# The four down projections of a diffusion backbone by seven products of quarter blocks instead of eight, the sums for them on GpSimd

## The chip, the cores and the metric

The program runs on one core of a Trainium2 chip. The metric is the device time of one launch in microseconds. The kernel before was timed in three runs, the kernel after is timed the same way. One further execution of the kernel before was taken with the hardware profiler; all rows below come from that one.

## The reference, cut to what matters

The model has two layers of three sub-layers each. The first and the last of a layer are SwiGLU blocks, the middle one is a mixer (in layer 0 a recurrence beside windowed attention, in layer 1 dense attention). The tokens are 512 latent tokens and 256 context tokens; the last sub-layer needs the 512 latent ones alone. D is 1024, D_FF 2816.

```
def _ffn_sublayer(h, shift, scale, gate, g_pre, g_post, w_gate, w_up, w_down):
    u = _modulate(_rmsnorm(h, g_pre), shift, scale)
    y = (jax.nn.silu(u @ w_gate) * (u @ w_up)) @ w_down
    return h + FFN_RES * gate * _rmsnorm(y, g_post)
...
for l in range(DEPTH):                      # DEPTH = 2
    x  = _ffn_sublayer(x, ..., ffn_w_gate[l, 0], ffn_w_up[l, 0], ffn_w_down[l, 0])
    xc = _ffn_sublayer(xc, ...)             # the context tokens, with the same weights
    x, xc = x + mixer..., xc + mixer...
    x  = _ffn_sublayer(x, ..., ffn_w_gate[l, 1], ffn_w_up[l, 1], ffn_w_down[l, 1])
    if not last: xc = _ffn_sublayer(xc, ...)
```

All is float32. The change concerns the four products `@ w_down` ([tokens, 2816] by [2816, 1024]); what prepares them is moved into the time of the products with `w_gate` and `w_up` just before.

## The kernel before, in words

The six sub-layers run one after the other, s = 0 to 5; s = 0, 2, 3 and 5 are the SwiGLU blocks. Tokens come in two chunks: 2 x 384 in s = 0, 2 and 3, 2 x 256 in s = 5.

A float32 product is three float32r passes on TensorE. Each operand is split into hi (a copy on ScalarE, ACT) and lo (the difference, on VectorE, DVE: a subtraction with both inputs in SBUF, lines L193 and L725), and hi*hi + hi*lo + lo*hi is summed in PSUM.

`ffn` is one SwiGLU block. The first two feature tiles (128 features each) are plain products (L200 to L202, `gu`). The other 20 are made by `strassen`, two tiles (a pair) at a time: for gate and for up one `job` of seven products (banks `px`, `py`, `pz`, L601), 84 matmuls. A job's weights (`w`, two loads of 512 KB on SyncE's queue, SP) are split, and sums of them are made on DVE (L614 to L617) and split again. DVE adds the products to what ACT has copied (L634), ACT applies Silu, DVE multiplies (L638). The finished pair h goes to DRAM (`hd<-h`).

The down projection is `type2`: 22 k-tiles; for each, w_down's 128 rows (512 KB) and a tile of h (`hr`) come from SP's queue and are split, and each token tile takes six matmuls of 512 columns (L701, accumulators `d000a` to `d110a`: layer, block, chunk, a). In s = 0, 2 and 3 it goes chunk by chunk; in s = 5 all four token tiles go together. The last four k-tiles (STAG) are done tile by tile, so that one token tile is finished while the others still run. For a finished tile, `boundary` takes the squares on ACT and the product with the gate G on DVE (L506), and makes 1/rms, its power step on GpSimd (POOL, L210); its `rest` loads x (a DMA on POOL's queue, L512), adds (DVE, L514), stores x (POOL's queue, L518) and calls `make_u`: POOL scales (L414), TensorE transposes (L419, `utp`), DVE and ACT modulate (L393, L395) and split (L193) into the next sub-layer's u. Where the next sub-layer is a SwiGLU block, `Sums` also makes four sums of u, half of them on POOL (L437, L451 and L453: operations with two inputs in SBUF) and half on DVE (L450, L452). The rests of the first chunk's tiles run beside the second chunk's products; those of the second chunk's run at the start of the next sub-layer.

What sets the order: each engine runs its instructions in a fixed order, which a scheduler makes from the order of the program and from when buffers come free. DMAs stand in the queue of the engine that issues them: one that waits holds up what stands behind it. Buffers that matter here: `raw` (weights as loaded) 3, hi and lo of weights 8 each, `c3` 23 slots of 3 KB a partition, `G0` and `G1` (the two gates, loaded before the down projection) one each, `by` 3, `junk` 1. PSUM has eight banks, of which the phases of the kernel (`psum_phase`) take six or eight.

## Time and profile before

| | us |
|---|---|
| median of three runs | 2626.99 (2625.99 to 2627.03) |
| span of the profiled execution | 2636.3 |
| TensorE (PE) busy in the span | 2546.2, 97% |
| VectorE (DVE) busy | 1757.5, 67% |
| ScalarE (ACT) busy | 1351.8, 51% |
| GpSimd (POOL) busy | 325.3, 12% |

The profiled execution is 9.3 us longer than the median of the timed runs. The stages of it that the change touches, in us from the start of the span: gate and up at 78 to 393, 981 to 1273, 1513 to 1804 and 2312 to 2501; down at 393 to 583, 1273 to 1463, 1804 to 1994 and 2501 to 2625. "Busy" is the time in which an engine executes instructions; an engine can be 67% busy on the mean and 99% in one stage, so rows are read by stage. "Idle before" is an engine's idle time ahead of an instruction, and the name after the arrow is what ended it.

### The profile page before, as it was taken

How to read it: one execution, taken by the hardware profiler on the slowest of the kernel's cores; microseconds unless marked ns; L12 is line 12 of the kernel's file. 1: busy time of each engine (PE TensorE's matmuls, PEld its weight loads, DVE VectorE, ACT ScalarE, POOL GpSimd, SP SyncE). 2: the span in 40 equal slices, each digit the busy share in tenths (PEclk: the TensorE clock that was granted, in tenths of full speed). 3: DMA queues.
4: the chain of work that ended last, by engine and by line, in shares of the span. 5: the costliest groups of instructions: out<-in, count | busy, mean ns of one | idle time of the engine just before them, and what ended most of it. 6: DMA issues, size and time to landing. Idle time of an engine off the chain costs nothing.

```text
span 2636.3 us, 38740 instructions
## 1 busy us (share of the span) xinstructions
PE 2546.2 (97%) x13980; PEld 2237.5 (85%) x13980; DVE 1757.5 (67%) x3199; ACT 1351.8 (51%) x2783; POOL 325.3 (12%) x356
## 2 busy tenths in 40 slices
PE   7999999999999999999999999999999899899998
PEld 5899998889855789999888899998887667799986
DVE  5766664658777686767555767665557657899843
ACT  4444444547566654444454544444545556666632
POOL 4000000213022240000011300000122221400000
PEclk8999999999999999999999999999999999999999
DMA  7445436541387443232555332235554552544542
GB/s 275 144 160 168 152 127 206 192 160 53 119 293 266 157 141 96 96 105 100 187 184 189 124 97 95 98 107 177 198 181 152 200 176 82 177 135 128 161 167 88
DMA packets 147761, 403.00 MB, mean 153 GB/s; under 512 B 16504, under 2 KB 33576, under 8 KB 147568
## 3 DMA queue, kind: packets, MB, share of 16 engines
q1 hardware_dynamic: 136688, 362.00, 41.6%
q0 software_dynamic: 10880, 38.53, 4.2%
q8 instruction: 109, 1.79, 0.3%
q14 instruction: 84, 0.69, 0.1%
HBM read 351.91 MB, written 48.55 MB: 152 GB/s over the span
## 4 chain that ended last, share of the span: by engine, by line
PE 80%; DVE 7%; issue 5%; ACT 3%; POOL 3%; DMA 2%; POOLq 0%; DVEq 0%; ACTq 0%; SPq 0%
PE px L601 17%; PE py L601 12%; PE pz L601 12%; PE d110a L701 4%; PE d100a L701 4%; PE d000a L701 4%; PE d010a L701 4%; PE ada L122 3%; PE d001a L701 3%; PE d101a L701 3%; PE eo0a L701 1%; PE oq1a L701 1%; PE qkv1a L701 1%; PE opT L1286 1%; PE gu L201 1%
## 5 line engine op out<-in xcount | busy, mean ns | idle before, releaser
L210 POOL TENSOR_TENSOR b_0pr<-b_0pv,mhalf 128x1 f32<-128x1 f32 x4 | 2.2, 560 | 983.9 <-DVE b_0pv L208 983.9
L634 DVE TENSOR_TENSOR cp<-px,cp 128x384 f32<-128x384 f32 (+1 forms) x160 | 76.5, 520 | 56.3 <-PE px L601 56.3
L724 ACT ACTIVATE hh<-hr 128x384 fp32r<-128x384 f32 x132 | 68.6, 521 | 81.5 <-DMA hr<-hd 80.6
L725 DVE TENSOR_TENSOR hh<-hr,hh 128x384 fp32r<-128x384 f32 x132 | 72.9, 559 | 50.6 <-ACT hh L724 49.5
L636 ACT ACTIVATE h<-cp 128x384 f32<-128x384 f32 (+1 forms) x160 | 77.0, 498 | 26.1 <-DVE cp L634 21.9
L122 PE MATMUL ada<-wa,sc 128*32 128x512 f32 x512 | 83.8, 611 | 0.5 <-DVE cols L137 0.4
L634 DVE TENSOR_TENSOR cp<-pz,cp 128x384 f32<-128x384 f32 (+1 forms) x80 | 41.9, 524 | 57.4 <-PE pz L601 56.4
L638 DVE TENSOR_TENSOR h<-cp,h 128x384 f32<-128x384 f32 (+1 forms) x160 | 79.6, 519 | 0.4
L629 ACT ACTIVATE cp<-px 128x384 f32<-128x384 f32 (+1 forms) x160 | 71.4, 446 | 0.0
L634 DVE TENSOR_TENSOR cp<-py,cp 128x384 f32<-128x384 f32 (+1 forms) x80 | 41.7, 521 | 26.7 <-PE py L601 17.2
L614 DVE TENSOR_TENSOR w<-w,w 128x512 f32<-128x512 f32 x80 | 56.8, 709 | 1.6 <-DMA w<-in_wgu_dram 0.2
L193 DVE TENSOR_TENSOR d110w_0lo<-d110w,d110w_0hi 128x512 fp32r<-128x512 f32 x22 | 15.2, 691 | 63.6 <-ACT d110w_0hi L193 63.6
L617 DVE TENSOR_TENSOR w<-w,w 128x512 f32<-128x512 f32 x80 | 55.3, 691 | 2.0
L615 DVE TENSOR_TENSOR w<-w 128x512 f32<-128x512 f32 x80 | 55.2, 690 | 1.9
L616 DVE TENSOR_TENSOR w<-w,w 128x512 f32<-128x512 f32 x80 | 55.1, 689 | 1.5
L701 PE MATMUL d011a<-d011w_0hi,hh 128*128 128x512 f32 x132 | 52.7, 399 | 0.2 <-ACT hh L724 0.2
L701 PE MATMUL d101a<-d101w_0hi,hh 128*128 128x512 f32 x132 | 52.5, 398 | 0.0
L701 PE MATMUL d001a<-d001w_0hi,hh 128*128 128x512 f32 x132 | 52.5, 398 | 0.0
L701 PE MATMUL d100a<-d100w_512hi,hh 128*128 128x512 f32 x132 | 52.4, 397 | 0.0
L701 PE MATMUL d000a<-d000w_512hi,hh 128*128 128x512 f32 x132 | 52.4, 397 | 0.0
L701 PE MATMUL d010a<-d010w_0hi,hh 128*128 128x512 f32 x132 | 52.3, 396 | 0.0
L701 PE MATMUL d101a<-d101w_512hi,hh 128*128 128x512 f32 x132 | 52.2, 396 | 0.0
(5579 smaller groups left out, 9579.9 us busy)
## 6 DMA issues: line engine op xcount, KB each, us to landing
w<-in_wgu_dram SPq DMA_DIRECT2D x175, 512.0 KB, 3.5
wa<-in_w_ada_dram SPq DMA_DIRECT2D x204, 256.0 KB, 4.6
hd<-h SPq DMA_DIRECT2D x66, 384.0 KB, 4.7
hr<-hd SPq DMA_DIRECT2D x132, 192.0 KB, 3.7
wa<-in_w_ada_dram SPq DMA_DIRECT2D x42, 512.0 KB, 4.3
d000w<-in_w_down_dram SPq DMA_DIRECT2D x22, 512.0 KB, 3.5
d001w<-in_w_down_dram SPq DMA_DIRECT2D x22, 512.0 KB, 3.8
d010w<-in_w_down_dram SPq DMA_DIRECT2D x22, 512.0 KB, 3.9
```

What stands on the lines that cost most here:

```text
L122: ins = nc.tensor.matmul(acc[32 * g:32 * g + 32, :], lhsT=self.sc[:, k, :], rhs=raws[g], start=(k == 0), stop=(k == KD - 1), skip_group_ch ...
L601: mm = lambda x, y, **kw: nc.tensor.matmul(out, lhsT=x, rhs=y, skip_group_check=True, **kw)
L614: nc.vector.tensor_sub(x3, x1, x3)
L615: nc.vector.tensor_add(x1, x1, x2)
L617: nc.vector.tensor_sub(x4, x4, x2)
L629: nc.scalar.activation(t, src, AF.Copy)
L634: nc.vector.tensor_add(t, acc, t)
L636: nc.scalar.activation(hc, t, AF.Silu)
L638: nc.vector.tensor_mul(hc, t, hc)
L701: mm(acc[:, h:min(h + 512, n)], lhsT=x[xi][:, js], rhs=w[h // 512][wi], start=(k == 0 and xi == 0 and wi == 0), stop=(k == nk - 1 and xi = ...
L724: self.nc.scalar.activation(t[:, 0], src, AF.Copy)
L725: self.nc.vector.tensor_sub(t[:, 1], src, t[:, 0].bitcast(F32))
```

## The change

A pair of feature tiles of h, by the two chunks of tokens, is a block of 2 x 2: a11 and a21 are the first tile's features for the first and second chunk, a12 and a22 the second tile's. The two tiles' rows of w_down, by halves of 512 columns, are the other: b11, b12 the first tile's, b21, b22 the second's. The result has four quarters (chunk by half of D). The old way needs eight products of such blocks, the new seven (Strassen's scheme in Winograd's form), each summed over the 11 pairs.

- `down_sums` loads a pair's rows of w_down a second time (into the places of `G0` and `G1`) during gate and up, makes b12 - b11, b22 - b12, b22 - b12 + b11 and b21 less that by four POOL subtractions of 128x512, and stores them (two DMAs of 512 KB on POOL's queue) to `wt` in DRAM.
- `h_sums` makes a21 + a22, a11 - a21, a21 + a22 - a11 and a12 less that by four POOL operations of 128x384 (128x256 in s = 5) and stores them with three DMAs on POOL's queue; a12 and a22 are stored by SP. Before, SP stored both tiles.
- `down` is new: seven products, each of 11 pairs by m token tiles (3, or 2 in s = 5) by three matmuls of 512 columns. Weights and h are loaded two pairs at a time. Of the PSUM banks, products 1, 3, 6 and 7 use `dx` and products 2, 4 and 5 `dy`; partial results are copied to SBUF by ACT (`keep`) and added by DVE (`add`, one input in PSUM). In products 6 and 7 the lo halves of h are made on POOL for two of three loads.
- `boundary` is split: `half` is done for each half of D when it is ready, `end` makes 1/rms. The first chunk's left half is ready after product 2, its right half after product 5; the rests of the first chunk run during products 6 and 7. The second chunk's tiles are finished in product 7, STAG now counts pairs.
- In s = 5 the down projection also goes by the two chunks of 256 tokens.

```
+    def down_sums(self, l, s, p, wt):
+        b = [self.bp.tile([P, D], F32, tag=f"G{e}", name=f"wt{l}{s}{p}{e}") for e in range(2)]
+        for e in range(2):
+            nc.sync.dma_start(b[e], self.a["w_down"][l, s, (2 * p + e) * P:(2 * p + e + 1) * P, :])
+        (b11, b12), (b21, b22) = ((x[:, 0:512], x[:, 512:]) for x in b)
+        sub = nc.gpsimd.tensor_sub
+        sub(b11, b12, b11)
+        sub(b12, b22, b12)
+        nc.gpsimd.dma_start(wt[p, 0], b[0])
+        sub(b22, b22, b11)
+        sub(b21, b21, b22)
+        nc.gpsimd.dma_start(wt[p, 1], b[1])
+
+    def h_sums(self, h, n, hd, nm):
+        a11, a21, a12, a22 = (x[:, c * n:(c + 1) * n] for x in h for c in range(2))
+        nc.sync.dma_start(hd[1], h[1])
+        s12 = self.bp.tile([P, 2, n], F32, tag="by", bufs=3, name=f"hs{nm}")
+        s4 = self.junk(f"hs{nm}")[:, 0:n]
+        nc.gpsimd.tensor_add(s12[:, 0], a21, a22)
+        nc.gpsimd.tensor_sub(a21, a11, a21)
+        nc.gpsimd.dma_start(hd[0], h[0])
+        nc.gpsimd.tensor_sub(s12[:, 1], s12[:, 0], a11)
+        nc.gpsimd.dma_start(hd[2], s12.rearrange("p c n -> p (c n)"))
+        nc.gpsimd.tensor_sub(s4, a12, s12[:, 1])
+        nc.gpsimd.dma_start(hd[3][:, 0:n], s4)
...
+        def product(a, b, acc, first, done):
...
+            for p in range(np_):
+                if i > 4 and p % 2 and self.later:
+                    self.later.pop(0)()
...
+                if p % 2 == 0:
+                    w = min(2, np_ - p)
...
+                    br = self.ws.tile([P, w, 512], F32, tag="raw", bufs=3, name=f"dw{nm}{p}")
+                    nc.sync.dma_start(br, b(q))
+                    ar = self.c3([P, w, n], F32, f"dh{nm}{p}")
+                    nc.sync.dma_start(ar, a(q))
...
+                    self.halves(ah, al, ar, nc.gpsimd if i > 4 and p % 4 else nc.vector)
+                wh, wl = self.split(br[:, p % 2], f"dw{nm}{p}s")
...
+        product(blk(0, 0), raw(0, 0), x, True, keep(u1))
+        product(blk(1, 0), raw(1, 0), y, True, add(u1, left))
...
+        product(blk(2, 1), mod(1, 1), x, False, keep(u2))
...
+        product(blk(2, 0), mod(0, 0), z, True, keep(c22))
+        product(blk(3, 0), raw(1, 1), z, False, add(u2, right))
+        product(blk(0, 1), mod(0, 1), x, False, add(c22))
+        product(blk(1, 1), mod(1, 0), x, False, second)
...
         for p in range(1, NF // 2):
             h = [self.c3([P, 2 * n], F32, f"h{l}{s}_{2 * p + e}") for e in range(2)]
+            self.down_sums(l, s, p, wt)
             for b in range(2):
                 job(p, b, h)
-            for e in range(2):
-                nc.sync.dma_start(hd[2 * p + e], h[e])
-        self.psum_phase(joint)
+            self.h_sums(h, n, hd[p], f"{l}{s}{p}")
```

What this does to the order of POOL's instructions in the last sub-layer's gate and up: before, POOL made the last sums of u there (L451, L453 for token tile 5) and after them had only the gates' load and the down projection's boundaries.

```order
L451 TENSOR_TENSOR b4_5y_21756<-b4_5uut_21779 128x512
L453 TENSOR_TENSOR b11_5_21620<-b11_5_21620,b01_5_21619 128x512
L167 DMA G17_0_24908<-gd17_20986 128x1024
L210 TENSOR_TENSOR b5_2pr_25732<-b5_2pv_25730,mhalf_71 128x1
L512 DMA b5_4x_25818<-xd4_19063 128x1024
```

After, at the same place (pairs are numbered in the names: `hs110` and `hd11` are the sums of h's pair 0 and their place in DRAM, `wt1120` and `wt1121` the two weight tiles of pair 2):

```order
L607 DMA hd11_22160<-hs110_22459 128x512
L608 TENSOR_TENSOR hs110q_22460<-h11_1_22254,hs110_22459 128x256
L609 DMA hd11_22160<-hs110q_22460 128x256
L588 TENSOR_TENSOR wt1120_22776<-wt1120_22776 128x512
L589 TENSOR_TENSOR wt1120_22776<-wt1121_22777,wt1120_22776 128x512
L590 DMA wt11_22161<-wt1120_22776 128x1024
L591 TENSOR_TENSOR wt1121_22777<-wt1121_22777,wt1120_22776 128x512
L592 TENSOR_TENSOR wt1121_22777<-wt1121_22777 128x512
L593 DMA wt11_22161<-wt1121_22777 128x1024
L588 TENSOR_TENSOR wt1130_23074<-wt1130_23074 128x512
```

So POOL now holds a chain of subtractions and stores for each pair. The scheduler puts the weight sums early: those of pairs 0 and 1 stand ahead of the first sums of h, and in each of the next pairs two follow, so that nine of the eleven are made in the first half of the stage. The other three SwiGLU blocks have the same pattern, there starting beside the boundary work of the mixer or block before.

On SP's queue in the same stage, before (`w113`, `w114` are the gate and up weights of pairs 3 and 4, `hd11<-h11_4` a store of h):

```order
L174 DMA w11310_22803<-in_wgu_dram 128x1024
L174 DMA w11311_22805<-in_wgu_dram 128x1024
L662 DMA hd11_21806<-h11_4_22383 128x512
L174 DMA w11400_22945<-in_wgu_dram 128x1024
L662 DMA hd11_21806<-h11_5_22384 128x512
L174 DMA w11401_22947<-in_wgu_dram 128x1024
```

and after:

```order
L174 DMA w11310_23222<-in_wgu_dram 128x1024
L585 DMA wt1150_23670<-in_w_down_dram 128x1024
L585 DMA wt1151_23671<-in_w_down_dram 128x1024
L174 DMA w11311_23224<-in_wgu_dram 128x1024
L174 DMA w11400_23382<-in_wgu_dram 128x1024
L585 DMA wt1160_23968<-in_w_down_dram 128x1024
L600 DMA hd11_22160<-h11_5_22775 128x512
L585 DMA wt1161_23969<-in_w_down_dram 128x1024
L174 DMA w11401_23384<-in_wgu_dram 128x1024
```

Loads of gate and up weights (`w11311`, `w11401`) now stand behind loads of `wt`, and a load of `wt` can only start when POOL's store of the weight sums before it has left the same buffer.

## Rows read from the trace of the kernel before

**Rows 1.** The page: busy time by engine, and the chain's shares by engine
```profile
PE 2546.2 (97%) x13980; PEld 2237.5 (85%) x13980; DVE 1757.5 (67%) x3199; ACT 1351.8 (51%) x2783; POOL 325.3 (12%) x356
...
PE 80%; DVE 7%; issue 5%; ACT 3%; POOL 3%; DMA 2%; POOLq 0%; DVEq 0%; ACTq 0%; SPq 0%
```
**Rows 2.** Stretches start:end; each engine's busy us; PEclk, DMA share, GB/s
```profile
393.00:485.00 92.00, 92.00 (x396) 74.13 (x395) 48.95 (x86) 42.12 (x82) 2.08 (x3) 1.00 0.59 192
1365.00:1463.00 98.00, 96.56 (x430) 77.62 (x429) 57.41 (x99) 50.08 (x102) 25.27 (x25) 1.00 0.56 185
2501.00:2625.00 124.00, 123.41 (x528) 99.07 (x528) 47.13 (x80) 37.07 (x71) 2.84 (x5) 1.00 0.40 135
```
**Rows 3.** Stretches with gate and up; columns PE, PEld, DVE, ACT, POOL
```profile
1513.00:1804.00 291.00, 291.00 (x1649) 291.00 (x1649) 196.80 (x330) 137.74 (x258) 0.00 (x0) 1.00 0.30 99
2270.00:2300.00 30.00, 25.79 (x213) 24.89 (x212) 26.16 (x53) 16.97 (x42) 15.68 (x15) 1.00 0.46 150
2300.00:2501.00 201.00, 198.53 (x1679) 197.72 (x1678) 183.29 (x343) 129.60 (x268) 0.00 (x0) 1.00 0.44 139
2312.00:2332.00 20.00, 20.00 (x172) 20.00 (x171) 18.64 (x35) 12.93 (x28) 0.00 (x0) 1.00 0.47 148
```
**Rows 4.** POOL's timeline in three places: start us, us, instruction
```profile
66.23 2.23 POOL L483 TENSOR_TENSOR zt<-zt,zt 128x768 f32<-128x768 f32 x1 [1.96 <-DVE zt L482]
...
945.27 1.33 POOL L453 TENSOR_TENSOR b<-b,b 128x512 f32<-128x512 f32 x1
...
961.79 3.37 POOL L451 TENSOR_TENSOR b_5y<-b_5uut 128x512 f32<-128x512 f32 x1 [0.93 <-DVE b_5uut L393]
```
**Rows 5.** DVE's timeline in the same three places
```profile
66.68 2.34 DVE L614 TENSOR_TENSOR w<-w,w 128x512 f32<-128x512 f32 x1
...
945.38 0.69 DVE L506 TENSOR_TENSOR b_5y<-eo1a,G 128x512 f32<-128x512 f32 x1
...
962.12 1.29 DVE L193 TENSOR_TENSOR u_1l<-b_5uut,u_1h 128x512 fp32r<-128x512 f32 x2
963.33 0.69 DVE L452 TENSOR_TENSOR b<-b_5uut,b_5y 128x512 f32<-128x512 f32 x1
```
**Rows 6.** Single lines, ns minimum/median/maximum of one, first and last start
```profile
L193 DVE TENSOR_TENSOR d011w_0lo<-d011w,d011w_0hi x22: 674/692/1781, 1361.6 to 1444.9; 128x512 fp32r<-128x512 f32 x22
L453 POOL TENSOR_TENSOR b<-b,b x8: 1262/1286/1409, 945.3 to 2290.7; 128x512 f32<-128x512 f32 x8
L437 POOL TENSOR_TENSOR b<-u_0h,u_0l x16: 1282/1596/2876, 910.9 to 2258.8; 128x512 f32<-128x512 f32 x16
```
**Rows 7.** DVE's additions from PSUM by form, 2312 to 2491
```profile
L634 DVE TENSOR_TENSOR cp<-px,cp 128x256 f32<-128x256 f32 x38 | 14.4, 420 | 3.1 <-PE px L601 3.1
L634 DVE TENSOR_TENSOR cp<-pz,cp 128x256 f32<-128x256 f32 x18 | 7.6, 421 | 1.0
L634 DVE TENSOR_TENSOR cp<-py,cp 128x256 f32<-128x256 f32 x18 | 7.5, 418 | 0.0
```
**Rows 8.** Two stretches of 10 us behind the third sub-layer's down projection
```profile
1473.00:1483.00 10.00, 6.75 (x37) 6.42 (x36) 6.69 (x10) 2.76 (x6) 6.52 (x6) 0.88 0.51 188
1493.00:1503.00 10.00, 10.00 (x59) 10.00 (x58) 9.96 (x24) 6.75 (x18) 0.00 (x0) 1.00 0.25 98
```
**Rows 9.** PE's waits at 1463 to 1513: total us, times, longest
```profile
PE b_5utp L419 <- POOL b_5y L414: 3.2, 1, 3.2
```
**Rows 10.** The chain there: start us, us, what
```profile
1464.56 1.21 DVE b_4x L514
...
1475.16 1.29 DVE b_5x L514
...
1481.67 1.97 PE b_5utp L419 x8
```
**Rows 11.** DMA issues: KB each, median us to landing; a store's time on POOL
```profile
w<-in_wgu_dram SPq DMA_DIRECT2D x175, 512.0 KB, 3.5
hd<-h SPq DMA_DIRECT2D x66, 384.0 KB, 4.7
hr<-hd SPq DMA_DIRECT2D x132, 192.0 KB, 3.7
xd<-b_2x POOLq DMA_DIRECT2D x5, 512.0 KB, 3.0
...
1455.48 0.59 POOL L518 DMA_DIRECT2D xd<-b_3x  x1 [1.62 <-DVE b_3x L514]
```

More of the change, by code (lines that the diff above doesn't have):

```diff
@@ L521, in boundary, with half, end, rest @@
-        return rest
+        def half(i, y):
+            nc.scalar.activation(junk[:, cut[i]], y, AF.Square, accum_out=ss[:, i:i + 1])
+            nc.vector.tensor_mul(y1[:, cut[i]], y, g[:, cut[i]])
+        def end():
+            nc.vector.tensor_add(ss[:, 0:1], ss[:, 0:1], ss[:, 1:2])
+            r = self.rms_r(ss[:, 0:1], D, name + "p")
+            def rest():
+                x = bp.tile([P, D], F32, tag="bx", bufs=2, name=name + "x")
+                nc.gpsimd.dma_start(x, xsrc(t))
+                for c in cut if nxt is None else [slice(0, D)]:
+                    nc.vector.scalar_tensor_tensor(x[:, c], y1[:, c], r[:, 0:1], x[:, c], op0=ALU.mult, op1=ALU.add)
+                    if nxt is None:
+                        nc.sync.dma_start(xdst(t)[:, c], x[:, c])
+                if nxt is not None:
+                    nc.gpsimd.dma_start(xdst(t), x)
+                    self.make_u(x, y1, t, *nxt, name + "u")
+            return rest
@@ L524, in ffn_weights, with ffn @@
+        return half, end
     def ffn_weights(self, l, s, f):
         return [self.weights(self.a["wgu"][l, s, f, b], f"w{l}{s}{f}{b}") for b in range(2)]
-    def ffn(self, l, s, u, sums, tiles, gate, finish, hook=None, joint=False):
+    def ffn(self, l, s, u, sums, tiles, gate, start, finish, hook=None, joint=False):
         nc = self.nc
         n = len(tiles[0]) * P
-        hd = self.dp.tile([NF, P, 2 * n], F32, name=f"hd{l}{s}")
+        hd = self.dp.tile([NF // 2, 4, P, 2 * n], F32, name=f"hd{l}{s}")
+        wt = self.dp.tile([NF // 2, 2, P, D], F32, name=f"wt{l}{s}")
@@ L567, in ffn @@
                     sums.most()
[L568 to L570 removed]
+        self.down_sums(l, s, 0, wt)
+        self.h_sums([h[0], h[1]], n, hd[0], f"{l}{s}0")
+        self.strassen(l, s, u, sums, n, hd, wt, joint)
         self.flush()
[L572 to L586 removed]
@@ L588, in strassen @@
-    def strassen(self, l, s, u, sums, n, hd, joint):
+        self.down(l, s, n, hd, wt, self.load_gate(*gate), start, finish, hook)
+    def down_sums(self, l, s, p, wt):
+        nc = self.nc
+        b = [self.bp.tile([P, D], F32, tag=f"G{e}", name=f"wt{l}{s}{p}{e}") for e in range(2)]
[9 more added lines that the diff above has]
+        nc.gpsimd.dma_start(wt[p, 1], b[1])
@@ L591, in strassen @@
+    def strassen(self, l, s, u, sums, n, hd, wt, joint):
         nc = self.nc
@@ L1335, in fin @@
                     self.later.append(sn.prepare)
+            def fin(c, j, acc, g, start=start, finish=finish):
+                half, end = start(c, j, g)
+                for i in range(2):
+                    half(i, acc[:, i * 512:(i + 1) * 512])
+                finish(c, j, end)
             if sub == 1:
@@ L1338, in body @@
             else:
-                self.ffn(l, sub // 2, u, sums, tl[s], gate, fin, {0: self.even_consts, 3: self.odd_consts}.get(s), s == 5)
+                self.ffn(l, sub // 2, u, sums, tl[s], gate, start, finish, {0: self.even_consts, 3: self.odd_consts}.get(s), s == 5)
             u, sums, xsrc = un, sn, dst
```

102 lines of the change are left out of this document (66 added, 36 removed).

## The prediction

> **What bounds the kernel now.** I read the page first: PE is busy 97% of the span, DVE 67%, POOL 12%, and PE holds 80% of the chain that ended last [rows 1]. So PE's matmuls set the time on the mean. Then I read the windows of the stages that the change touches. In a down projection PE is full (92.00 of 92.00 us for 396 matmuls; 123.41 of 124.00 for 528 in the last sub-layer) and DVE half idle [rows 2]. In gate and up with 384 tokens a chunk PE is again full and DVE at 196.80 of 291.00 us, POOL at nothing. But in the last sub-layer, with 256 tokens, DVE has 183.29 of 201 us, and 18.64 of 20 in one pair of feature tiles: there PE and DVE are nearly level, and the pair has no room [rows 3]. What the reader is to see is that the change takes work from PE in stages where PE alone is the bound, and puts POOL work into stages in one of which the bound is almost DVE. Last I read what POOL's two-input operations do to DVE, in three places.
>
> **Removed matmuls.** A sub-layer's down projection with 768 tokens has 22 x 6 x 6 = 792 matmuls of 512 columns; the seven products have 7 x 11 x 3 x 3 = 693, so 99 fewer. At 92.00/396 = 0.232 us [rows 2] this is 23.0 us, three times. The last has 528, then 7 x 11 x 2 x 3 = 462: 66 x 0.234 = 15.4 us. Together -84.4 us. It counts in full, since PE has no idle time there. The cover needed in its place: two pairs bring 512 KB of weights and 256 KB of h in 12 matmuls, 2.8 us, in the last sub-layer, that is 280 GB/s; the same stretch moved 135 GB/s at a DMA share of 0.40 [rows 2], so 0.83 of the engines. With 384 tokens it is 896 KB in 4.2 us, less. I cost the loads at nothing; 10% short in the last sub-layer would be +11 us.
>
> **What POOL's sums do to DVE.** When POOL runs a subtraction with two inputs in SBUF, a DVE instruction that also has two in SBUF is held: at 66.23 POOL's L483 takes 2.23 us, and DVE's L614 beside it takes 2.34, where L193 of the same size takes 0.692 (median), and that line's longest is 1.781, 1.09 more [rows 4 to 6]. A DVE instruction that reads PSUM is not: L506 takes 0.69 beside POOL's L453 of 1.33. It also goes the other way: at 961.79 POOL's L451 took 3.37 us while DVE ran such instructions one behind the other [rows 4, 5]. Alone, the POOL operation takes 1.29 us (L453, median), beside DVE 1.60 (L437, median) [rows 6].
>
> [...]
>
> Last sub-layer: 11 pairs, each with four POOL operations of 512 columns and four of 256. Held time per operation: 1.09 us for 512, for 256 half of it, 0.55. In all 11 x (4.36 + 2.2) = 72 us if every one is held for its full length. DVE can do something else meanwhile only when the next instruction in its order reads PSUM: L634's additions are 14.4 + 7.6 + 7.5 = 29.5 us [rows 7]. I take three quarters held (54 us), between all and the 0.6 that perfect packing with those additions would leave. From 2270 to 2501 DVE is busy 26.16 + 183.29 = 209.5 of 231 us, so 21.5 are free [rows 3]. 54 - 21.5 = **+32 us**. Bounds: +21 (209.5 - 29.5 + 72 - 231, the additions all beside POOL) and +50 (72 - 21.5); the far ends are 0, should POOL slip into DVE's gaps alone, and +72, should none of the free time be usable.
>
> The other three gate and ups: DVE is free for 94 of 291 us [rows 3], that is 9.4 per pair, and the hold is 4 x 1.09 + 4 x 0.82 (384 columns) = 7.6 per pair; early, two weight sums fall into a pair, 4.4 more, so 12 against 9.4 for the first half of the stage. What spills over is mostly taken up by the weights being loaded ahead. I take **+3** (1 each; bounds 0 and 8 each, five pairs of 1.6 too much).
>
> The start of s = 0, 2 and 3 gets the first weight sums too. It is where DVE has least room: 9.96 of 10 us at 1493 to 1503 [rows 8]. Two weight sums there hold 2 x 4 x 1.09 = 8.7 us at most; half of it, **+12** (4 each, bounds 0 and 8.7).
>
> **Products 6 and 7** now share their time with the first chunk's rests, which before ran beside a whole chunk's product of 92 us. Two products last 2 x 99 x 0.234 = 46.4 us. DVE there: 22 weight splits of 0.69 and the six h splits left to it, of 768 columns at 1.04 at most, together 21; additions 5; rests of three tiles some 13 (an estimate from L514's 1.2 us [rows 10] and splits of 0.69); 39 in all, and POOL's six h splits (768 columns) and the sums of u hold it for about 16: 55 against 46.4. Some of it moves behind the products. I take **+12** (4 each; bounds 0 and 10).
>
> **Tails.** The second chunk's three tiles now end in product 7 alone, the last four pairs tile by tile: a tile has 4 x 3 x 0.232 = 2.8 us, where before it had 4 x 6 x 0.232 = 5.6. A tile's rest is slower than either: L514 of tile 4 stands at 1464.56 and that of tile 5 at 1475.16, and the last transposes at 1481.67, 6.5 us behind [rows 10]. [...] Two tiles that come 2.8 us closer need 5.6 us more of other work for PE, of which the next sub-layer's first products give some: **+9** (3 each, bounds 0 and 7: all of it, and a clock that falls). In the last sub-layer nothing follows the tail, its half tile is shorter too, nothing.
>
> **First products.** The first product of a down projection needs all 11 pairs of h only near its end, 25 us in, but its first load stands behind the last pair's chain of four POOL operations and three stores on POOL's queue. A store lands 3.0 to 4.7 us after its issue and a load 3.7 [rows 11]. Hidden but for the last pairs: **+2** (bounds 0 and 10).
>
> **The sum.** -84.4 + 32 + 3 + 12 + 12 + 9 + 2 = -14.4 us. Against the profiled span of 2636.3 that is 2621.9; this execution stands 9.3 us above the median of the runs, 2626.99, so **2613 us** for the timed runs. The likeliest case by itself reaches from 2590 (last sub-layer at +21, each of the 12 a third lower, nothing spilled) to 2638 (+50 and a little more at the starts).
>
> **Rivals.**
> A, faster: the hold is mostly hidden. POOL takes the shared inputs only in DVE's gaps and beside its PSUM reads: last sub-layer at +21, no spill, 4 in all for the starts, 4 for products 6 and 7, 4 for the tails, 1 for the first products: -84.4 + 34 = -50, 2577 us. With no hold at all (POOL and DVE not in each other's way, against the 2.34 us of L614) only the terms 12, 9 and 2 are left: -61, 2566 us; that has 0.04 of A's chance. For it speaks that L506 went through undelayed [rows 5]; against it that L437's 16 operations have a median 0.3 us above L453's, so they do collide [rows 6].
> B, slower: the hold counts in full. The last sub-layer at +50, the three other stages at 16 together, starts 24, products 6 and 7 24, tails 9, first products 6: +129 - 84.4 = +45, 2672 us. Its place is DVE's queue in the last gate and up, its price 1.09 us per operation of 512 columns, and it decides once about nine in ten are held. For it speak 18.64 of 20 us in a pair [rows 3], against it the 29.5 us of additions from PSUM [rows 7].
> C, slower: POOL's chain holds SP's queue. The weights of the next pair stand behind a load of `wt`, which waits until POOL's store has left the buffer. One weight sum's chain is a load of 3.5 us, three POOL operations up to the second tile's store's issue, 0.59, and a landing of 3.0 [rows 11]: with 1.6 us per operation 11.9, two of them 23.8 in a pair's 29.1 us. Beyond 2.5 us per operation two no longer fit; L451 has taken 3.37 [rows 4]. At 2.9 it is 31.6 per pair: 2.5 over for some 4.5 pairs in three sub-layers, 34 us, and in the last (19.8 us a pair) its eleven weight chains and sums of h overrun by some 21 beyond the 32 above. -14.4 + 55 = +41, 2668 us. Against it: the three raw buffers are loaded ahead, and the median is 1.60.
>
> **How the numbers follow.** Forecast case 0.42, A 0.22, B 0.20, C 0.16. What a measurement of this kernel can tell from no change is 0.2%, that is 2621.7 to 2632.2 us. Of the forecast case I put 0.28 on faster, 0.10 on no change and 0.04 on slower. Faster: 0.28 + 0.22 = 0.50; same 0.10; slower 0.04 + 0.20 + 0.16 = 0.40. For 8 in 10, I go from 2565 (a little beyond A, the loss of the two hold terms) to 2678 (a little beyond B).
>
> **What the profile after would show.** Right: 363 fewer matmuls on PE and down projections of 161 and 108 us of matmuls; in the last gate and up, DVE at 95% or more with L193 and L614 to L617 longer than 0.69 us beside POOL, and PE with some 30 us of idle time there, waiting for DVE's lo halves; the other gate and ups within 3 us of before. Wrong: L614 to L617 at their old mean (then A), PE waits in the 384-token stages that end with loads of `w` (then C), or more than 12 us idle in a block's products 6 and 7, which would make that place the dearest. If the last gate and up gets longer by less than 15 or by more than 60 us, my measure of the hold is wrong.

## The result, and the profile after

The kernel after takes 3048.08 us (median; 3044.22 to 3054.95), the kernel before beside it 2626.49 us: a ratio of 1.159 [1.156, 1.162]. The change costs 422 us. The forecast was 2613 us with a range to 2678; it was wrong in direction and in size.

The profiled execution after spans 3053.1 us, 416.8 more than before's. Its page has, for the busy times of [rows 1]:

```profile
PE 2616.8 (86%) x13617; PEld 2252.0 (74%) x13617; DVE 2107.7 (69%) x3222; ACT 1408.3 (46%) x2830; POOL 955.7 (31%) x952
```

The 363 matmuls are gone (13980 less 13617), and yet PE is busy 71 us longer: the granted clock of the whole execution is 0.93, where before's is 0.99. The records of both traces hold two levels, 1.00 and 0.50, so PE ran at the lower one more often. Then the same windows as before, by stage. Two of before (the third sub-layer's gate and up, and its down projection), and below them four of after (the same two, then those of the last sub-layer); columns as in [rows 2]:

```profile
982.00:1273.00 291.00, 291.00 (x1681) 290.95 (x1680) 201.98 (x339) 141.64 (x267) 0.00 (x0) 1.00 0.32 103
1273.00:1463.00 190.00, 188.56 (x824) 151.86 (x823) 104.38 (x180) 90.58 (x180) 27.35 (x28) 1.00 0.56 185
```
```profile
1069.00:1429.00 360.00, 307.83 (x1683) 304.34 (x1682) 269.06 (x342) 140.69 (x268) 126.63 (x126) 0.93 0.44 156
1429.00:1651.00 222.00, 186.97 (x719) 142.27 (x717) 118.97 (x167) 98.24 (x169) 40.46 (x36) 0.90 0.54 184
2600.00:2859.00 259.00, 216.54 (x1678) 210.17 (x1676) 248.34 (x348) 125.32 (x267) 129.18 (x130) 0.93 0.59 201
2861.00:3040.00 179.00, 132.00 (x462) 93.70 (x461) 83.39 (x127) 71.88 (x130) 15.69 (x18) 0.90 0.52 171
```

Read the first column against the second. With the same matmuls (1681 and 1683 lie in the two windows), gate and up went from 291 to 360 us: PE is idle for 52 and, at a granted clock of 0.93, busy 17 longer. In the down projection PE has 105 instructions less in its window, 24.4 us at the old rate, but 187 us for what would be 164: 23 us at the lower clock (0.90 on the mean), and 35 idle on top. DVE's 269 us instead of 202 are for nearly the same instructions (342, 339); that POOL holds them is seen below.

Stages from their first to their last matmul (plain first features, gate and up, down projection; us, before and after; measured like this, gate and up of sub-layer 3 begins at 1507 and that of sub-layer 5 at 2300 in the trace of before):

| sub-layer | start | gate and up | down |
|---|---|---|---|
| 0 | 48.2, 58.9 | 314.6, 354.2 | 190.1, 218.6 |
| 2 | 41.4, 44.4 | 291.4, 360.1 | 190.6, 221.8 |
| 3 | 44.2, 50.5 | 297.0, 353.3 | 190.1, 229.9 |
| 5 | 43.0, 43.3 | 200.6, 259.5 | 123.5, 179.1 |
| sum | +20.3 | +223.5 | +155.1 |

Of the rest, 18 us, 12 lie in the mixers and 3 between sub-layers 2 and 3. Since 84.4 us of matmuls left the down projections, their own loss is 155 + 84 = 240 us, a little more than that of gate and up. In these eight stages PE is idle 331 us, where it was 8.

What PE waits for in gate and up. The waits of SP's queue and of PE in the third sub-layer's stage (us in total, times, longest):

```profile
SPq L585 <- DMA wt<-wt: 109.6, 16, 12.2
```
```profile
PE pz L716 <- ACT cp L744: 49.3, 10, 13.8
```

SP's queue stands still for 110 us behind loads of w_down's rows whose place POOL's store still reads; gate and up weights stand behind them. At the longest wait of PE (13.8 us, until 1212.34), SP's queue and ACT:

```profile
1196.16 5.22 SPq L585 DMA_DIRECT2D wt<-in_w_down_dram  x2
1201.49 0.85 SPq L174 DMA_DIRECT2D w<-in_wgu_dram  x2
```
```profile
1206.48 0.63 ACT L193 ACTIVATE 0141a22hi<-w 128x512 fp32r<-128x512 f32 x1 [12.15 <-DMA w<-in_wgu_dram]
```

The weights that ACT has to split are issued at 1201.49, behind the two `wt` loads, and ACT stands still for 12.2 us until they are there. In ACT's order the Silu and the copy that frees the bank `pz` come behind that split, and the Silu waits another 3.8 us for DVE. POOL's timeline earlier in the stage:

```profile
1094.58 1.28 POOL L589 TENSOR_TENSOR wt<-wt,wt 128x512 f32<-128x512 f32 x1 [4.53 <-DMA wt<-in_w_down_dram]
1096.15 0.55 POOL L590 DMA_DIRECT2D wt<-wt  x1 [0.30 <-POOL wt L589]
1096.73 1.30 POOL L591 TENSOR_TENSOR wt<-wt,wt 128x512 f32<-128x512 f32 x1
1098.11 1.64 POOL L592 TENSOR_TENSOR wt<-wt 128x512 f32<-128x512 f32 x1
1100.04 0.56 POOL L593 DMA_DIRECT2D wt<-wt  x1 [0.30 <-POOL wt L592]
1106.46 1.29 POOL L588 TENSOR_TENSOR wt<-wt 128x512 f32<-128x512 f32 x1 [5.86 <-DMA wt<-in_w_down_dram]
1108.71 1.29 POOL L589 TENSOR_TENSOR wt<-wt,wt 128x512 f32<-128x512 f32 x1 [0.96 <-DMA wt<-in_w_down_dram]
```

From one L589 to the next are 14.1 us here, of which POOL works 6.6 and waits 6.8 for the loads. Over eight weight sums (their stores L590 from 1046.39 to 1178.13) it is 16.5 us each.

Later in the stage, without these waits, PE stops for 2 us once in each pair (six times from 1246 to 1407). The four engines at one such place, PE first:

```profile
1279.09 0.44 PE L716 MATMUL pz<-u_1h,0160s4hi 128*128 128x384 f32 x1 [2.01 <-ACT cp L744]
```
```profile
1277.62 0.52 ACT L751 ACTIVATE h<-cp 128x384 f32<-128x384 f32 x1 [4.15 <-DVE cp L749]
1278.05 0.61 ACT L193 ACTIVATE 0161s1hi<-w 128x512 fp32r<-128x512 f32 x1
1278.57 0.47 ACT L744 ACTIVATE cp<-pz 128x384 f32<-128x384 f32 x1
```
```profile
1270.67 1.51 DVE L193 TENSOR_TENSOR 0161a11lo<-w,0161a11hi 128x512 fp32r<-128x512 f32 x1
1272.10 1.50 DVE L193 TENSOR_TENSOR 0161a12lo<-w,0161a12hi 128x512 fp32r<-128x512 f32 x1
1273.52 1.50 DVE L729 TENSOR_TENSOR w<-w,w 128x512 f32<-128x512 f32 x1
1275.06 2.06 DVE L730 TENSOR_TENSOR w<-w 128x512 f32<-128x512 f32 x1
1277.04 0.55 DVE L749 TENSOR_TENSOR cp<-py,cp 128x384 f32<-128x384 f32 x1
```
```profile
1270.37 1.26 POOL L603 TENSOR_TENSOR hs<-h,h 128x384 f32<-128x384 f32 x1 [25.93 <-DVE h L753]
1271.71 1.34 POOL L604 TENSOR_TENSOR h<-h 128x384 f32<-128x384 f32 x1
1273.01 1.47 POOL L606 TENSOR_TENSOR hs<-hs,h 128x384 f32<-128x384 f32 x1
...
1275.53 1.03 POOL L608 TENSOR_TENSOR hs015q<-h,hs 128x384 f32<-128x384 f32 x1
```

POOL's four sums of h hold four DVE instructions in a row (1.5 to 2.1 us instead of 0.69). DVE's addition L749, of 0.55 us, stands behind them; ACT's Silu L751 waits for it, ACT's copy L744 that frees the bank `pz` stands behind the Silu, and PE waits for the bank. Before, DVE had 30% of the stage free; PE loses 2 us all the same.

In the down projection, SP's queue, ACT and PE at the first such wait:

```profile
448.39 0.37 SPq L640 DMA_DIRECT2D dw<-in_w_down_dram  x1
448.87 0.41 SPq L642 DMA_DIRECT2D dh<-hd  x1
452.75 0.97 SPq L640 DMA_DIRECT2D dw<-in_w_down_dram  x2
453.83 0.46 SPq L642 DMA_DIRECT2D dh<-hd  x1
```
```profile
464.12 0.84 ACT L193 ACTIVATE dh0008h<-dh 128x768 fp32r<-128x768 f32 x1 [8.14 <-DMA dh<-hd]
```
```profile
465.02 0.79 PE L661 MATMUL dx<-dw0008shi,dh0008h 128*128 128x512 f32 x1 [6.04 <-ACT dh0008h L193]
```

The load of h that is needed at 459 is issued at 453.83, behind two loads of weights that in the order of SP's queue are for pairs 2 to 5 of the next product, and arrives after 10 us. Its place in the queue is not all of that. The DMA engines come in bursts there (columns as in [rows 2]; the last three are the granted clock, the DMA share and GB/s):

```profile
453.00:458.00 5.00, 5.00 (x23) 4.06 (x22) 2.49 (x4) 1.89 (x3) 0.26 (x1) 1.00 1.00 366
458.00:464.00 6.00, 0.97 (x5) 0.44 (x3) 0.00 (x0) 0.00 (x0) 0.00 (x0) 0.85 0.96 365
464.00:470.00 6.00, 4.98 (x13) 3.72 (x14) 2.63 (x4) 2.91 (x5) 0.00 (x0) 0.58 0.32 109
470.00:476.00 6.00, 4.85 (x21) 3.58 (x19) 2.04 (x3) 3.60 (x6) 0.00 (x0) 1.00 0.05 13
```

From 453 to 464 they are full (1.00 and 0.96), and PE stands still from 459 on; from 470 to 476 they have nearly nothing to do (0.05), since the next load of weights waits in SP's queue until a place is free (7.2 us). The stage's mean share of 0.54 shows neither. The same waits for the hi half of h stand at most products' starts and ends: in the last sub-layer PE waits 24 times for one, 0.3 to 3.5 us each.

By products: the first five of a block last 146 to 149 us in the three blocks with 768 tokens, for matmuls of 115 (0.232 us each), and are idle for 20 to 21; products 6 and 7 last 70, 75 and 84 us for matmuls of 46 and are idle for 14, 14 and 28.

### The profile page after: what moved, and what is told of

Its sections match the earlier page's. It is cut to its first block, busy times and chain, and to the rows that moved or that the text cites. A ratio compares the mean times of both kernels' runs of the same rounds, so it can differ in the third digit from the quotient of the medians.

```text
span 3053.1 us, 39181 instructions
## 1 busy us (share of the span) xinstructions
PE 2616.8 (86%) x13617; PEld 2252.0 (74%) x13617; DVE 2107.7 (69%) x3222; ACT 1408.3 (46%) x2830; POOL 955.7 (31%) x952
## 5 line engine op out<-in xcount | busy, mean ns | idle before, releaser
L603 POOL TENSOR_TENSOR hs<-h,h 128x384 f32<-128x384 f32 (+1 forms) x44 | 48.9, 1112 | 584.2 <-DVE h L753 579.5
L751 ACT ACTIVATE h<-cp 128x384 f32<-128x384 f32 (+1 forms) x160 | 75.5, 495 | 184.8 <-DVE cp L749 169.9
L729 DVE TENSOR_TENSOR w<-w,w 128x512 f32<-128x512 f32 x80 | 93.7, 1171 | 75.5 <-DMA w<-in_wgu_dram 74.5
L589 POOL TENSOR_TENSOR wt<-wt,wt 128x512 f32<-128x512 f32 x44 | 74.2, 1685 | 123.1 <-DMA wt<-in_w_down_dram 123.1
L749 DVE TENSOR_TENSOR cp<-px,cp 128x384 f32<-128x384 f32 (+1 forms) x160 | 76.2, 517 | 40.9 <-PE px L716 40.6
L730 DVE TENSOR_TENSOR w<-w 128x512 f32<-128x512 f32 x80 | 99.2, 1240 | 1.9
L753 DVE TENSOR_TENSOR h<-cp,h 128x384 f32<-128x384 f32 (+1 forms) x160 | 96.3, 622 | 0.4
L588 POOL TENSOR_TENSOR wt<-wt 128x512 f32<-128x512 f32 x44 | 64.2, 1458 | 87.0 <-DMA wt<-in_w_down_dram 86.9
L1204 POOL TENSOR_SCALAR p<-p,sm 128x256 f32<-128x256 f32 (+2 forms) x48 | 31.8, 674 | 133.6 <-DVE sm L1200 52.8
L749 DVE TENSOR_TENSOR cp<-pz,cp 128x384 f32<-128x384 f32 (+1 forms) x80 | 41.6, 520 | 44.3 <-PE pz L716 44.2
L744 ACT ACTIVATE cp<-px 128x384 f32<-128x384 f32 (+1 forms) x160 | 71.3, 446 | 0.0
L732 DVE TENSOR_TENSOR w<-w,w 128x512 f32<-128x512 f32 x80 | 69.4, 868 | 2.0
L731 DVE TENSOR_TENSOR w<-w,w 128x512 f32<-128x512 f32 x80 | 68.0, 850 | 1.5
L592 POOL TENSOR_TENSOR wt<-wt 128x512 f32<-128x512 f32 x44 | 67.7, 1538 | 3.1
L606 POOL TENSOR_TENSOR hs<-hs,h 128x384 f32<-128x384 f32 (+1 forms) x44 | 59.8, 1359 | 0.0
L591 POOL TENSOR_TENSOR wt<-wt,wt 128x512 f32<-128x512 f32 x44 | 57.5, 1306 | 0.9
L604 POOL TENSOR_TENSOR h<-h 128x384 f32<-128x384 f32 (+1 forms) x44 | 56.6, 1286 | 3.2
L1391 POOL TENSOR_SCALAR op<-op,osm 128x768 f32<-128x768 f32 x32 | 30.4, 952 | 76.1 <-DVE osm L1390 50.9
L749 DVE TENSOR_TENSOR cp<-py,cp 128x384 f32<-128x384 f32 (+1 forms) x80 | 41.3, 516 | 15.9 <-PE py L716 15.9
```

What stands on the lines that cost most here:

```text
L588: sub(b11, b12, b11)
L589: sub(b12, b22, b12)
L592: sub(b21, b21, b22)
L729: nc.vector.tensor_sub(x3, x1, x3)
L730: nc.vector.tensor_add(x1, x1, x2)
L731: nc.vector.tensor_add(x2, x3, x2)
```

## The experiments

G and D are the sums of the four gate and up and the four down stages in the profile of each run, measured as above. Kernels that are alike in gate and up read G from 1249 to 1278, so a difference under 30 us in G alone means little; D is 844 to 859 in six runs whose down projections are alike (after, e_wtq, e_wt_off, e_both_off, f_dvesums, h_hdve).

| run | median us | ratio to before | G | D |
|---|---|---|---|---|
| before | 2626 to 2631 | 1 | 1104 | 694 |
| after | 3048 | 1.159 [1.156, 1.162] | 1327 | 849 |
| e_wtq | 2984 | 1.136 [1.134, 1.139] | 1249 | 848 |
| e_wt_off | 2896 | 1.102 [1.100, 1.104] | 1188 | 855 |
| e_both_off | 2794 | 1.063 [1.060, 1.067] | 1095 | 844 |
| e_hq | 3010 | 1.146 [1.143, 1.150] | 1311 | 815 |
| f_dvesums | 2905 | 1.105 [1.102, 1.107] | 1183 | 859 |
| f_hq2 | 2915 | 1.109 [1.106, 1.112] | 1272 | 768 |
| f_stag2 | 2964 | 1.127 [1.122, 1.132] | 1275 | 826 |
| f_dvesplit | 2964 | 1.128 [1.124, 1.132] | 1278 | 825 |
| g_onein | 3137 | 1.192 [1.186, 1.198] | 1310 | 897 |
| h_onein | 2900 | 1.103 [1.101, 1.106] | 1141 | 867 |
| h_hdve | 2964 | 1.127 [1.123, 1.130] | 1229 | 850 |
| g_ahead | 2869 | 1.092 [1.087, 1.096] | 1264 | 724 |
| h_ahead2 | 2857 | 1.086 [1.079, 1.092] | 1270 | 709 |
| g_best | 2710 | 1.031 [1.028, 1.034] | 1143 | 576 (three) |

**e_wtq.**
```
-            nc.sync.dma_start(b[e], self.a["w_down"][l, s, ...])
+            nc.gpsimd.dma_start(b[e], self.a["w_down"][l, s, ...])
```


> The second loads of w_down's rows (for the weight sums) are issued from POOL's queue instead of SP's; nothing else is changed. Theory Q (the gate and up stages lose their time because SP's queue stands still behind these loads, 110 us of waiting for POOL's stores in the third sub-layer's stage): the gaps of 8 to 14 us in the first half of the 384-token stages go, with the time at the lower clock behind them; each of these stages gets 25 to 45 us shorter, the whole about 100 to 140 us, to 2910 to 2950. Theory L (it is DVE held by POOL's two-input subtractions): the same subtractions run, so the time stays at 3048 within 25 us.

64 us less, where Q expected 100 to 140, so Q has a part, about half of what it claimed: the third sub-layer's stage falls from 360 to 319 us, the last stays (259.5 and 262). The rest is another cause.

**e_wt_off.** `down_sums` is not called, `mod = raw`.

> Leaves out the sums of the weights altogether (no second load, no subtraction, no store; the seven products read plain rows of w_down in their place, in loads of the same size and shape). Theory Q: as with the loads on POOL's queue, within 30 us of that run. Theory L: 176 of 352 subtractions of the two kinds are gone, the larger ones, so 60% of the loss in gate and up (some 135 us) goes here and nothing in the run with the loads on POOL's queue. If both have a part: that run takes the big gaps, and this one another 30 to 60 us, most of it in the last sub-layer's 260 us.

The products then read plain rows of w_down. 88 us less than e_wtq, 47 of them in the last sub-layer's stage (262 to 215), 15 in the other three and 20 at the starts: both theories have a part.

**e_both_off.**
```
-        nc.gpsimd.tensor_add(s12[:, 0], a21, a22)
-        nc.gpsimd.tensor_sub(a21, a11, a21)
         nc.gpsimd.dma_start(hd[0], h[0])
...
+        nc.gpsimd.dma_start(hd[2], h[0])
+        nc.gpsimd.dma_start(hd[3][:, 0:n], a12)
```


> Leaves out the sums of the weights and the four POOL operations on h (the stores of h stay, of unsummed tiles). Gate and up should come back to before's 314, 291, 297 and 201 us within 5 each if POOL's work and its queue are all of their loss (224 us), whatever Q and L share: about 2825 us. What is then left against before is the down projections' own loss: 165 us longer than before instead of 84 shorter, if it does not hang on the sums. If the down projections also get shorter here by more than 30 us, they were waiting for the sums' stores.

314, 291, 291 and 198 us, as expected (the third 6 us shorter); the total, 2794, is 31 below the 2825 expected, 16 of it at the starts. Its window in the third sub-layer (PE, PEld, DVE, ...) is before's:

```profile
1012.00:1303.00 291.00, 291.00 (x1680) 291.00 (x1680) 201.57 (x337) 141.58 (x265) 15.55 (x29) 1.00 0.35 121
```

So the stores and the other phases of PSUM cost nothing there; POOL's sums and the loads and stores of `wt` are all of the loss in gate and up. The down projections do not hang on them (D 844).

**e_hq.**
```
-                nc.sync.dma_start(ar, a(q))
+                nc.gpsimd.dma_start(ar, a(q))
```


> In the seven products the loads of h are issued from POOL's queue, so that they no longer stand behind loads of weights for later products in SP's queue. Theory S (their place in SP's queue makes them late): the waits of 3 to 6 us for the hi half of h at the ends and starts of the products go, a 768-token down projection gets 25 to 45 us shorter and the last one 40 to 60, together 120 to 190 us, so 2860 to 2930. Theory D (the DMA engines, or the places for h in SBUF, are the limit): no change within 25 us. Against a gain also speaks that in products 6 and 7 the loads would stand behind POOL's own work; then these two products get longer by 10 us or more while the first five get shorter.

Only 34 us of D, and 38 of the whole, between the two theories. The loads then wait for places (43 us of POOL's time before loads of h in the first block); what remained at that block's product starts was 1.9 us each.

**f_dvesums.** On e_wtq, `nc.vector` in place of `nc.gpsimd` for all eight sums.

> All eight subtractions and additions of a pair (weights and h) on DVE instead of POOL; the second loads of w_down from POOL's queue, as in the run at 2984 us. Theory L (what is left of the loss in gate and up is DVE held by POOL): in the 384-token stages DVE has 94 of 291 us free and gets 11 x (4 x 0.69 + 4 x 0.53) = 54 us of work, so each comes back to within 15 us of before's 314, 291, 297 (from 340, 319, 328: 45 to 75 us less in all); in the last, DVE's 183 + 50 us do not fit in 201, so it stays at 235 to 260 us. Total 2900 to 2940. Rival (the loss is the extra latency between h, its sums and the buffers, whoever makes them): no gain beyond 20 us.

337, 308, 304 and 234 us: 67 us of G go and the total is in theory L's range, but only one of the three 384-token stages comes to within 15 us of before. 79 us are left, also where DVE has room (239 of 308 us busy in the third sub-layer). The additions that free the banks stand behind the sums in DVE's order just as behind held instructions: at 160.27 in this run L749 comes behind L604, L606 and L608, ACT has waited 3.3 us for it, and PE then waits 2.1 for the bank.

**f_hq2.**
```
-                    ar = self.c3([P, w, n], F32, f"dh{nm}{p}")
-                    nc.sync.dma_start(ar, a(q))
-                    ah, al = (self.c3([P, w, n], F32R, f"dh{nm}{p}{e}") for e in "hl")
+                    al = self.c3([P, w, n], F32R, f"dh{nm}{p}")
+                    ar = al.bitcast(F32)
+                    nc.gpsimd.dma_start(ar, a(q))
+                    ah = self.c3([P, w, n], F32R, f"dh{nm}{p}h")
```


> On the run at 2984 us: the seven products load h from POOL's queue, and the lo half takes the place of the loaded tile, so a load of two pairs needs two places of the 23 instead of three. With the loads on POOL's queue alone the down projections took 211, 214, 228 and 162 us (from 219, 222, 230, 179), and there the loads waited for places. Theory S+D (queue order and places together): 185 to 200 us each and 140 to 150 in the last, total 2880 to 2930. Rival (what is left is the order of the products' ends on ACT, where the copies of a finished product stand ahead of the next product's hi halves, 1.9 us each): 208 to 215 and 155 to 162, total 2940 to 2960.

202, 205, 220 and 140 us: between the two for 768 tokens, the theory's for the last. Queue and places together are 80 us of D. In the block of 220 PE waits 21.1 us once, for a load of h in product 6.

**f_stag2.** `p < np_ - 2` for `p < np_ - self.STAG`, on e_wtq.

> On the run at 2984 us: only the last two pairs of a product go token tile by token tile, not four, so that half as many halves of weights (8 places each) and of h are held until a product's end. Theory W (the prefetch of the next product is limited by these places at each product's end): the waits of 3 to 6 us at the product starts go down by half, 10 to 20 us a down projection, total 2920 to 2950. Theory S (loads of h stand behind loads of weights in SP's queue): the order there is the same, so no change within 15 us; the second chunk's tiles then end 1.4 us apart instead of 2.8, which may cost 2 to 5 us in the tails.

D is 21 us less: 6 to 11 us shorter in each block with 768 tokens, 6 longer in the last. A small part.

**f_dvesplit.** `self.halves(ah, al, ar)` on e_wtq.

> On the run at 2984 us: the lo halves of h in products 6 and 7 are made on DVE, not on POOL. In these products PE waits for `dh..52l` (2.7 us), `b_2y` (4.9) and `dh..56` (2.9, in one block 15.1), all of them POOL's or behind it. Theory P (POOL's queue, splits among boundary work, is the bound of products 6 and 7): 10 to 15 us a block, 40 in all, total 2940 to 2955. Rival (the boundary's chain is the bound, whoever splits): no change within 15 us.

POOL makes every second of these lo halves, three of a product's six (not two of three, as the change was described above). D is 22 us less, 17 of them in one block. There POOL's split stood behind the building of tables for the next mixer (L1246), and PE waited 15.1 us for it; elsewhere the rival holds.

**g_onein.**
```
+        one = lambda o, i: nc.gpsimd.tensor_scalar(o, i, self.mhalf[:, 0:1], None, op0=ALU.mult)
-        sub(b11, b12, b11)
-        sub(b12, b22, b12)
+        one(b[0], b[0])
+        one(b[0], b[0])
...
```


> On the run with the second loads on POOL's queue (2984 us): each of POOL's eight sums of a pair is replaced by an operation with one input (a scaling of the whole tile, 1024, 768 or 384 columns, so of about the same length), in the same places, with the same buffers, loads and stores; the sums themselves are left out. Theory L2 (DVE is held only by POOL operations with two inputs in SBUF): gate and up come back to within 10 us of before's 314, 291, 297 and 201 (from 340, 319, 328 and 262), 120 to 150 us less, total 2835 to 2865. Rival H (the stages lose because h, its sums and their buffers stay occupied longer, or because POOL takes SBUF's time whatever it does): at most a third of that, total 2935 or more.

It could not tell: this operation took 3.03 us (mean, 1024 columns), twice the sum that it replaced, and the chain of POOL, so lengthened, became a bound by itself (3137 us): in the third sub-layer's stage ACT waits 39.7 us in three pieces, up to 18.4, for stores of h on POOL's queue (`DMA hd<-h`), and PE twice 15 to 16 us.

**h_onein.** The same with `1.0, op0=ALU.mult, op1=ALU.mult`.

> As the run g_onein, but with the scaling in the form that the kernel uses elsewhere (two multiplications in one operation; 1024 columns took 1.1 us, 768 took 0.95 there), so that an operation has about the length of the sum that it replaces (1.3 to 1.6 us), not twice that. Theory L2 (DVE is held only by POOL operations with two inputs in SBUF): gate and up 1100 to 1140 us in all instead of 1249, DVE's sums of the gate and up weights at 0.69 to 0.80 us instead of 0.87 to 1.15, total 2840 to 2890. Rival H (the chain through POOL's queue and the buffers, whoever is held): 1200 us or more, total 2935 or more.

G is 1141, the end of the theory's range: 109 of the 154 us above e_both_off go, with as many POOL operations of about the same length (means of 0.99 to 1.53 us for 768 and 1024 columns, where seven of the eight sums in e_wtq took 1.29 to 1.61). DVE's busy time in the third sub-layer's stage, e_wtq first, then h_onein:

```profile
1058.00:1377.00 319.00, 301.33 (x1681) 297.45 (x1680) 264.63 (x343) 141.67 (x269) 137.67 (x143) 0.98 0.51 177
```
```profile
1031.00:1335.00 304.00, 296.66 (x1681) 295.70 (x1680) 233.95 (x342) 141.64 (x268) 120.63 (x129) 0.99 0.50 173
```

DVE is held 32 us there instead of 63, so two inputs on POOL's side matter, but "only" is wrong: half of the hold remains. The sign that theory L2 named did not come either: DVE's sums of the gate and up weights took 0.78 to 1.03 us (means of the four lines over the run), not 0.69 to 0.80. Besides, the first two one-input operations on a pair need only one of its two loads, where the second sum needs both, so a shorter chain may have a part in the 109 us; no run separates the two. The whole, 2900, misses its range, since D grew by 19; why was not followed up.

**h_hdve.** The four lines of `h_sums` with `nc.vector`, on e_wtq.

> On the run at 2984 us: the four sums of h on DVE, the four of the weights stay on POOL. By the stages so far POOL's sums of h cost 12.7, 30.4, 32.8 and 16.6 us in the four stages, and all sums on DVE 22, 17, 12 and 34. If what hurts is four POOL operations in a row on h, right where DVE's additions release the PSUM banks: each 384-token stage comes to within 25 us of before, total 2910 to 2940. Rival (DVE is held the more by the weights' sums, which are longer): less than 25 us won, 2960 or more.

20 us less in the time (the intervals of the two runs do not meet) and in G, where 20 is within the scatter; two of the three 384-token stages stay 32 us above before: the rival. That the sums of the weights by themselves do most of what both do is not shown, since here DVE has the sums of h to make.

**g_ahead.** Loads and splits of a pair are made by `emit(t)`, called one load ahead:
```
+                if p % 2 == 0:
+                    if i == p == 0:
+                        emit(0)
+                    emit(flat.index((i, p)) + 1)
+                e = ent.pop((i, p))
```


> On the run that loads h from POOL's queue and makes lo in its place (2915 us, down projections 202, 205, 220, 140): each load of two pairs, its splits too, stands in the program one load ahead of the matmuls, over the ends of the products as well, and the lo halves in products 6 and 7 are made on DVE. Theory A (what is left at the product starts, 1.94 us each, is ACT's order: the hi half of the next product's h stands behind the copies of the finished one): these gaps go, and with the splits off POOL the gaps of 5 us in products 6 and 7 too; 180 to 190 us each and 120 to 128 in the last, total 2840 to 2865. Rival (DMA capacity, or the lower clock by itself): less than 15 us in all, 2900 or more.

188, 193, 203 and 139 us: the gaps at the product starts are gone, 44 us of D, a little less than expected; the last sub-layer did not gain. In the block of 203 PE still waits 22.6 us once in product 6: there it is a load of h that stands in POOL's queue behind the building of the tables, as the split did in the kernel after.

**h_ahead2.** `(nc.sync if i > 4 else nc.gpsimd).dma_start(ar, a(q))`.

> On the run with the loads ahead (2869 us): in products 6 and 7 the loads of h go through SP's queue again, not through POOL's, where they stand behind the boundaries' operations. If that is the rest of these products (a wait of 4 to 6 us for the hi half of h in each block), the 768-token down projections come to 178 to 190 us from 188, 193 and 203, total 2840 to 2858. Rival (the boundary's own chain, `b_2y` and the transposes, or the queue of SP): no change within 10 us.

189, 188, 186 and 146 us, in the expected range: it helps the one block of 203 by 17 us and the others by little or nothing (the times of the two runs, 2857 and 2869, are too close to tell apart). The matmuls would be done in 161 us at 0.232 us each, or 167 at the pace of before's whole stage; a window of one of these blocks shows what is left, 15 us idle and a clock of 0.95:

```profile
431.00:620.00 189.00, 174.48 (x718) 137.29 (x717) 119.75 (x204) 99.45 (x175) 45.21 (x60) 0.95 0.63 211
```

The first five products now last 124 us, 9 above their matmuls; products 6 and 7 still 61 to 65 us for matmuls of 46.

**g_best.** g_ahead with the sums on DVE, and with the eight products of before in the last sub-layer.

> The run with the loads ahead, all sums on DVE, and the last sub-layer by the way of before (eight products, four token tiles at a time, no sums). By the stages seen so far: gate and up 336, 308, 304 and 201 (+45 us against before), starts +10, down projections 180 to 190 each against 190 (0 to -30 in all), the last as before: 2640 to 2690 us. It beats before only if the down projections come under 172 us each; I put 0.15 on that.

2710 us, 20 above its range, and 3% slower than before. Gate and up cost 39 us more than before, the three down projections (184, 191, 201) gain nothing, the rest is spread over mixers, starts and the passage between sub-layers 2 and 3. No version was found that beats the kernel before.

## Why the prediction was wrong

**Removed matmuls, -84.4.** Right: 363 fewer. "It counts in full, since PE has no idle time there" is the sentence that failed: with the matmuls gone, the four stages got 155 us longer. It holds only while loads and splits keep their old lead (one load ahead, with the lo halves on DVE, took D from 768 to 724).

**"I cost the loads at nothing."** The dearest error: the down projections lost about 240 us against terms of 23 (products 6 and 7, tails, first products). I compared bytes with the rate that the DMA engines reach. On the mean the rate was enough (0.54 and 0.52 of the engines are busy); in the bursts it was not (0.96 to 1.00), and the lead was too short to bridge them. A load of h stands in SP's queue behind loads of weights for later pairs, each of which waits for a place; it needs three of 23 places, and per matmul twice as many bytes of h are loaded as before (384 KB, not 192, for 18). f_hq2 took 80 us of D away and the runs with loads ahead 125 to 140, without changing a byte; the latter also make the lo halves on DVE, which by itself took 22.

**Other three gate and ups, +3.** Measured +40, +69 and +56. Two steps failed. First, I set held time (7.6 us a pair) against DVE's free time (9.4). The held time was sized well: DVE's 67 us more in the third sub-layer are 0.8 of the 84 for eleven pairs. But free time elsewhere in the pair pays for nothing when PE's bank hangs on one addition behind four held instructions (a wait of 2.0 us at 1279.09). (The upper bound also had a slip: 12 against 9.4 is 2.6 too much a pair, so 13 us for five pairs and not 8; the measured times lie beyond either.) Second, rival C was given 0.16, with 11.9 us for a weight sum's chain and a turning point at 2.5 us per POOL operation. The operations took 1.3 to 1.7 us, as I assumed, and the chain 16.5 us: I had counted POOL's work and the two transfers, and not that each load stands in a queue where the loads ahead of it wait in turn. e_wtq puts this queue at 78 us of G (49 by the highest of its likes), h_onein the two inputs of POOL's operations at 109 at most; 46 us are left between h_onein and e_both_off.

**Last gate and up, +32.** Measured +59; DVE is busy 248 of 259 us there, 65 more, so it is held for 0.9 of the 72 us. The hold was there, the share of three quarters was too low, and most of the free 21.5 us were not to be had. For this stage rival B, with its +50 at nine tenths held, came near; for the other three it had 16 us in all against 165. B and C together, not one of them, describe gate and up, and both had it too cheap there.

**Starts, products 6 and 7, tails, first products: +35.** The starts cost 20 with the last sub-layer's nothing, within their bounds. Products 6 and 7 were sized at 4 us a block, 10 at most, and cost 24, 29 and 38 beyond their matmuls; the sign named for it, more than 12 us idle in them, came in all three blocks (14, 14 and 28). In part it is POOL, as the term had it (4.9 us for `b_2y`, 15.1 for a split in one block), in part the late loads. Together they are 91 us, where the term had 12. What the tails and the first products cost was not measured apart.

**The lower clock** was priced only in the tails. In the trace of before it was 0.50 from 1481 to 1487, in the tail on which that price was put. After, it was 0.50 for about 7 us behind the wait of 6 us (0.58 on the mean from 464 to 470), 0.52 from 1204 to 1217 around the end of the wait of 13.8 us, and 0.57 from 1247 to 1251 behind one of 2.0 us that ended at 1246.12; behind the one that ended at 1279.09, as long, it was 1.00 until 1287. PE is idle 323 us more than before in the eight stages, which are 463 us longer for their matmuls, so by this difference, an estimate, some 140 us are the clock's.

On the hold itself, the trace of after shows again what [rows 4 to 6] showed: beside POOL's four sums, DVE's instructions with two inputs in SBUF took 1.5 to 2.1 us, and 0.68 to 0.69 from 1277.50 on, when the sums had ended. The runs add that POOL's side counts: with one-input operations the hold is half (32 us, not 63, in the third sub-layer's stage). What the two engines share, of which rival A speaks, no run shows; the hold alone was measured.

What stays open: the last 25 to 28 us of each 768-token down projection in h_ahead2 (15 to 19 of them in products 6 and 7), why D grew in both runs with one-input operations, and how far more DMA rate, rather than more lead, would have helped: no run changed it.

## What to carry to other kernels

Work taken from the engine that is the bound shortens a stage only if what feeds it was ahead by more than the new pace needs (here 363 matmuls went and the four down projections took 155 us more): compare lead (places times the time that each lasts) and the order in the queue, not only bytes per second on the mean. Idle time of an in-order engine is no budget for a burst (DVE had 30% of a stage free before, and PE lost 2 us in a pair behind it all the same): follow the instruction that frees the next PSUM bank and ask what will stand in front of it. And a load that waits for a store's end belongs in a queue where nothing else waits behind it (moved off SP's queue in e_wtq, 64 us less).

## What the runs showed of the hardware that was not expected

A scaling on POOL with one multiplication took 2.2 us and more for 768 columns, with two multiplications in the same instruction about 1 us in the same place (the two other scalings of 768 columns there: 2.4 and 2.5 us, against 1.2 and 1.5). The same line of the kernel, g_onein first, then h_onein (columns as in the page's part 5):

```profile
L603 POOL TENSOR_SCALAR h<-h,mhalf 128x768 f32<-128x768 f32 x33 | 74.7, 2264 | 228.1 <-DVE h L754 227.5
```
```profile
L603 POOL TENSOR_SCALAR h<-h,mhalf 128x768 f32<-128x768 f32 x33 | 32.7, 992 | 311.7 <-DVE h L754 311.0 <-DVE h L560 0.2
```

And DVE can pass a one-input POOL operation unharmed, but does not always: within POOL's one operation from 1290.53 to 1292.99 in g_onein, DVE's L193 took 1.24 us and the L730 behind it 0.68, where instructions of this kind took 1.5 to 2.1 beside sums. What decides between the two was not found.

```profile
1290.53 2.46 POOL L603 TENSOR_SCALAR hs<-hs,mhalf 128x768 f32<-128x768 f32 x1
```
```profile
1290.99 1.24 DVE L193 TENSOR_TENSOR 0161a12lo<-w,0161a12hi 128x512 fp32r<-128x512 f32 x1
1292.15 0.68 DVE L730 TENSOR_TENSOR w<-w,w 128x512 f32<-128x512 f32 x1
```
